# A hybrid decoder step on one core: where mixtures, inverses, the norm over heads and the residual's loads stand in their queues

## The chip, the cores and the metric

The kernel runs on one core of a Trainium2 chip. The metric is the device time of one execution in microseconds (us); lower is better. Before the change it is 2707.35 us, the median of three runs (2703.36 to 2710.01).

## The reference

One inference step of a two-layer decoder, all in float32: layer 0 mixes tokens with a causal convolution, layer 1 with an RWKV-7 recurrence, and each is followed by an MLP with squared ReLU. There is one prompt of 16 + 1024 tokens and a batch of 8 single tokens with states of their own. The part that matters here:

```python
def _rwkv7(h, ...):
    xx = prev - h                       # prev: h shifted by one token
    xr, xw, xk, xv, xa, xg = (h + xx * x_mix[i] for i in range(6))
    r, k, v = xr @ w_r, xk @ w_k, xv @ w_v
    ...                                 # decay, a, kk, gate g from small products
    S_final, ys = lax.scan(_wkv7_step, S0, xs)     # 64x64 state for each of 16 heads
    yn = (y - mu) * rsqrt(var + GN_EPS)            # norm over each head's 64 values
    out = ((yn + bonus) * g) @ w_o
    return out, h[:, -1], S_final

h = h + out
h = h + square(relu(rmsnorm(h) @ w_mlp_in)) @ w_mlp_out
```

## The kernel before, in words

Activations lie with features on the partitions and tokens along the free axis. Products of layer 0, of both MLPs and of `w_o` are made exact enough with three matmuls per 128x128 block: weights and activations are each split into a high part (a cast on ScalarE, L158 for weights `wi`, `wo`, L141 for activations) and a low part (a subtraction, on GpSimd L165 for weights, on VectorE L142 for activations); the matmuls are L190 to L192. Raw weights come through SP's DMA queue (L147), a few tiles ahead of use.

The program has these stages. (1) Layer 0's convolution and MLP for three groups of tokens, to about 1076 us. In the MLP, VectorE adds each finished bank `out` to the residual `h` (L357), and TensorE can't fill a bank again before that. (2) The projections of the recurrence layer, in four groups g of 272, 256, 256 and 264 tokens, to about 1750 us. `prepare(g)` loads the normalised rows `hx` (L861, L863) and forms `xx` (L868, two of three blocks on VectorE, the third on GpSimd); `mix` forms the mixture `mx` for one of the products and one block (L877). `keys(g)` makes the k products `pk` (L903), `mixer_in(g)` for each of 8 blocks p (two heads) the r and v products `pr`, `pv`, the small products `p_wa` (L974, L975), `l_w`, `l_a`, `l_g`, a scan over time of the decays (L1116) into `wa`, and the operands `ab` of the recurrence. PSUM banks of one kind come in a ring of four, those of the recurrence in a ring of three; a matmul waits for what reads the bank it takes.

(3) The recurrence in 17 chunks of 64 tokens (the first of 16), woven into stage 2 and the start of the last layer's MLP: for each chunk TensorE forms `A`, `gg`, `bT`, `W`, `po`, `U`, `S` and `Y` (L1236 to L1348), with VectorE and ScalarE between them. Each needs 32x32 triangular inverses, which `inverses(c, n)` (L1177 to L1209) works out for four chunks at once on VectorE: it loads `ni`, then alternates multiplications `tt` (L1197) and additions `ni` (L1200) on ever wider pieces. (4) For every two chunks, `norm_gate` (L1448 on): sums of `ey` over each head, mean and variance (L1459 to L1469), a transposition `yn` on TensorE (L1505), then gain, bonus and gate (L1484 to L1488) and a store to `d_z` (L1490). (5) `mixer_out(g)` for three groups of tokens of the last layer: products `ps_oo` of `z` with `w_o`, added to `h` (L1603) and squared (L252), and then the MLP.

The order is set by the order of the program, by a scheduler that moves instructions of all engines but TensorE, and by three kinds of hints. `kept_place(x)` keeps an instruction at its program position. `tc.issue_after(y)` queues an instruction behind a named one, `y`, of its engine. Generators stand for work that is woven in: `tick` takes one turn of the inverses, one of the recurrence and one of the norm, and each `yield` in them ends a turn, its number being a weight for `advance`. In stage 5 `filler` spreads three such streams over the points of the MLP: the rest of the recurrence (`until`), the decode step of the 8 single tokens, and the rest of the norm.

Memory comes from pools on a stack with two sides; a pool opened later on the same side gets what an earlier one gave back. The pool `wk` on the right holds the recurrence's tiles and also those of the norm. `lw.close()` gives it back; it stands behind the whole first MLP of the last layer with all its streams, and the residual `h` of groups 1 and 2 is loaded (`load_h`, L1581) into what it leaves. Four `wide` buffers hold the weights of the gate (`g`) and of the decay (`wa`), 24 `mixp` buffers the mixtures.

Of the kernel before, what the change touches and what calls it, by code (L numbers as in the profile page):

```python
# [16 lines left out]
P = 128  # L17
# [29 lines left out]
def hybrid_step(tc, x_prompt, x_sample, state_conv, state_shift, state_wkv, meta_tokens,  # L47
# [10 lines left out]
    with ctx:  # L58
# [244 lines left out]
        def filler(points, *streams):  # L303
# [10 lines left out]
            return fill, chain.from_iterable(it for it, _ in its)  # L314
        MLP_POINTS = 6 * DFF // P
# [5 lines left out]
        def mlp(layer, groups, lag, eng_w, eng_h, fill=None, done=None):  # L321
# [4 lines left out]
            hid = {}  # L326

# [9 lines left out]
            def inp(j, w, group):  # L337
# [5 lines left out]
                with tc.high_priority(offset=HR):  # L343
# [3 lines left out]
                    cur["low"] = split(hh[:, j % 2, :n], hl[:, j % 2, :n], s, eng_h)  # L347

            def out(b, i, w, group):
                gn, hv, n, ah, al, rs, hid_pool = group  # L350
                hh, hl = hid[gn, b]
                for m in range(4):
# [3 lines left out]
                    with tc.high_priority(offset=HA):  # L356
                        nc.vector.tensor_add(hv[:, 4 * i + m, :], hv[:, 4 * i + m, :], ps[:, :n])  # L357
# [422 lines left out]
        lw = ctx.enter_context(ExitStack())  # L780
        wk = pool(lw, "wk", 1, side="right")
# [30 lines left out]
        hnp = pool(ld, "hnp", 1)  # L812
        wide = pool(ld, "wided", 4)
        mixp = pool(ld, "mixp", 24)
# [14 lines left out]
        prep, norm, kept = {}, {}, {}  # L829
# [22 lines left out]
        def prepare(g):  # L852
# [13 lines left out]
            for k in range(KT):  # L866
                with nullcontext() if g else tc.issue_after(cur["low"].ins):
                    first = (nc.gpsimd if k % 3 == 2 else nc.vector).tensor_sub(xx[:, k, :npr], hx[:, k, 0:npr], hx[:, k, 1:1 + npr])  # L868
# [5 lines left out]
            def mix(i, k):  # L874

                t = mixp.tile([P, N1], F32, name=nm("mx", i, k), tag="mx")
                nc.vector.scalar_tensor_tensor(t[:, :n], xx[:, k, :n], vec("x_mix", i * KT + k), hx[:, k, 1:1 + n],  # L877
                                               op0=ALU.mult, op1=ALU.add)
# [59 lines left out]
        def mixer_in(g, tick):  # L938
# [140 lines left out]
            for p in range(KT):  # L1079
# [36 lines left out]
                nc.vector.tensor_tensor_scan(cum[:, :n], smask[:, :n], cum[:, :n], 0.0, op0=ALU.mult, op1=ALU.add)  # L1116
# [64 lines left out]
        def inverses(c, n):  # L1181
# [5 lines left out]
            (nc.sync if c else nc.gpsimd).dma_start(ni, blocks(d_n))  # L1187
            yield 5
            yield 1
            top = META if c == 0 else 32  # L1190
            every = 4 if c == 0 or c + n == NCH else 3 if c == 1 else 2
            aside = bank(f"tt{c}", "x")[:B] if c + n == NCH else None
            for j in range(top - 2, 0, -1):
# [3 lines left out]
                first = nc.vector.tensor_mul(o, ni[:, :j, j:j + 1].broadcast_to([B, j, wd]), ni[:, j:j + 1, j + 1:top].broadcast_to([B, j, wd]))  # L1197
                if j == top - 2:
                    kept_place(first)
# [10 lines left out]
        w_ = lambda shape, name, c, tag=None, bufs=1: wk.tile(shape, F32, name=f"{name}{c}", tag=tag or name, bufs=bufs)  # L1210
        kv = lambda t: t.rearrange("p (k v) -> p k v", k=KT)
# [60 lines left out]
        def chunk(c):  # L1272
# [67 lines left out]
            if c > 0:  # L1340
# [8 lines left out]
                ys[c] = w_([P, KT * HS], "ey", c, bufs=3)  # L1349
# [98 lines left out]
        def norm_gate():  # L1448
# [4 lines left out]
            def stats(y, n, name):  # L1453

                yv = y[:n].rearrange("t (h v) -> t h v", v=HS)
                ms = w_([P, 2, KT], "ems", name)
                sq = w_([P, KT * HS], "eq", name)
# [284 lines left out]
```

## Time and profile before

| | |
|---|---|
| median of three runs | 2707.35 us |
| profiled execution | 2701.97 us, its span 2700.3 us |
| granted TensorE clock, mean | 0.987 |
| TensorE busy | 2611.4 us, 97% |
| VectorE, ScalarE, GpSimd busy | 64%, 42%, 54% |
| DMA | 400.20 MB, 148 GB/s |

A row of a window shows its limits, its length, then the busy time of each engine with its number of instructions, the granted clock of TensorE (1.00 is full), the busy share of the DMA engines and what they moved. A row of a timeline shows start, time of one or several (x3) in a row, engine, line, operation and tiles, and in brackets how long the engine stood idle before it and what released it. A row of waits shows engine, what waited, for whom, and us in all, times, the longest. SPq is the queue of DMAs that SP issues; PE, DVE, ACT and POOL are TensorE, VectorE, ScalarE and GpSimd.

### The profile page before, as it was taken

Reading aid. Unit: us, or ns where it says so; the run is one execution under the profiler, and the core shown is the slowest. Engines: PE = TensorE matmul, PEld = TensorE weight load, DVE = VectorE, ACT = ScalarE, POOL = GpSimd, SP = SyncE. Lnnn points to the kernel's source line nnn. Section 1 sums busy time; section 2 is a strip of 40 time slices with the busy share of each in tenths; the row PEclk is TensorE's granted clock in tenths of the full one; section 3 lists DMA queues with packets and bytes.
Section 4 is the critical chain, followed back from the end, with each engine's and each line's share of the span. In section 5 each row is a group of like instructions: output and inputs, shape, how many; then the busy total and the mean of one; then the engine's idle time right before and its main releaser. Section 6 shows DMA issues by size and latency. Waiting matters only on the chain. (4 is left out here: it accounts for less than half of the span.)

```text
span 2700.3 us, 51347 instructions
## 1 busy us (share of the span) xinstructions
PE 2611.4 (97%) x19796; PEld 2455.6 (91%) x19796; DVE 1720.6 (64%) x3584; ACT 1134.6 (42%) x2099; POOL 1451.7 (54%) x2061
## 2 busy tenths in 40 slices
PE   9999999999999999998998999889999899999998
PEld 8999999999999999777887777789999899999998
DVE  6999999997444445344757476676679543334435
ACT  5546445445444333333344445445444442222223
POOL 7677878878887775022211113376678563333331
PEclk9999999999999999999999999999999999999999
DMA  6663544554456443568767867778655642222211
GB/s 187 175 167 108 161 145 134 155 175 133 141 160 187 138 141 107 171 196 211 198 175 188 213 154 194 189 197 191 154 163 175 178 124 70 71 71 71 64 54 44
DMA packets 602058, 400.20 MB, mean 148 GB/s; under 512 B 96128, under 2 KB 548928, under 8 KB 601814
## 3 DMA queue, kind: packets, MB, share of 16 engines
q1 hardware_dynamic: 573716, 359.95, 48.4%
q0 software_dynamic: 8768, 26.48, 3.1%
q10 hardware_dynamic: 19330, 10.49, 1.4%
q8 instruction: 156, 2.56, 0.4%
q14 instruction: 88, 0.72, 0.1%
HBM read 338.94 MB, written 58.83 MB: 147 GB/s over the span
## 5 line engine op out<-in xcount | busy, mean ns | idle before, releaser
L165 POOL TENSOR_TENSOR wo_lo<-wo_raw,wo_hi 128x256 fp32r<-128x256 f32 x736 | 540.7, 767 | 312.2 <-ACT wo_hi L158 302.7
L165 POOL TENSOR_TENSOR wi_lo<-wi_raw,wi_hi 128x256 fp32r<-128x256 f32 x640 | 472.1, 771 | 241.0 <-ACT wi_hi L158 235.5
L190 PE MATMUL out<-hh,wo_hi 128*128 128x352 f32 (+2 forms) x1536 | 498.7, 325 | 15.9 <-DVE h L357 11.4
L192 PE MATMUL ps_in<-m_l,wi_hi 128*128 128x352 f32 (+2 forms) x1536 | 492.9, 321 | 3.4 <-DVE m_l L288 3.4
L190 PE MATMUL ps_in<-m_h,wi_hi 128*128 128x352 f32 (+2 forms) x1536 | 494.5, 322 | 0.0
L357 DVE TENSOR_TENSOR h<-h,out 128x352 f32<-128x352 f32 (+2 forms) x768 | 385.8, 511 | 168.5 <-PE out L192 167.1
L191 PE MATMUL out<-hh,wo_lo 128*128 128x352 f32 (+2 forms) x1536 | 493.2, 321 | 0.0
L192 PE MATMUL out<-hl,wo_hi 128*128 128x352 f32 (+2 forms) x1536 | 492.1, 321 | 0.0
L191 PE MATMUL ps_in<-m_h,wi_lo 128*128 128x352 f32 (+2 forms) x1536 | 491.8, 320 | 0.0
L538 DVE SCALAR_TENSOR_TENSOR cv<-u,wdw,cv 128x348 f32<-128x348 f32 (+2 forms) x720 | 378.0, 575 | 0.7
L158 ACT CAST wi_hi<-wi_raw 128x1024 fp32r<-128x1024 f32 x160 | 167.7, 1049 | 386.9 <-PE out L192 192.6
L158 ACT CAST wo_hi<-wo_raw 128x1024 fp32r<-128x1024 f32 x184 | 192.6, 1048 | 325.5 <-PE out L192 166.2
L190 PEld LDWEIGHTS out<-hh,wo_hi 128*128 128x128 f32 x1536 | 289.8, 189 | 22.0 <-DVE h L357 13.7
L192 PEld LDWEIGHTS ps_in<-m_l,wi_hi 128*128 128x128 f32 x1536 | 288.6, 188 | 5.6 <-DVE m_l L288 5.2
L190 PEld LDWEIGHTS ps_in<-m_h,wi_hi 128*128 128x128 f32 x1536 | 289.5, 189 | 1.3
L191 PEld LDWEIGHTS out<-hh,wo_lo 128*128 128x128 f32 x1536 | 289.5, 188 | 0.8
L191 PEld LDWEIGHTS ps_in<-m_h,wi_lo 128*128 128x128 f32 x1536 | 289.1, 188 | 0.6
L192 PEld LDWEIGHTS out<-hl,wo_hi 128*128 128x128 f32 x1536 | 288.7, 188 | 0.0
L345 DVE SCALAR_TENSOR_TENSOR ps_in<-ps_in,rs_m 128x352 f32<-128x352 f32 (+2 forms) x192 | 100.6, 525 | 258.6 <-PE ps_in L192 258.3
L142 DVE TENSOR_TENSOR hl<-ps_in,hh 128x352 fp32r<-128x352 f32 (+2 forms) x192 | 98.8, 515 | 119.4 <-ACT hh L141 119.0
L346 ACT ACTIVATE ps_in<-ps_in 128x352 f32<-128x352 f32 (+2 forms) x192 | 85.1, 444 | 123.1 <-DVE ps_in L345 122.9
L903 PE MATMUL pv<-mx,wv_raw 128*128 128x256 f32 (+2 forms) x512 | 130.1, 403 | 1.1 <-ACT rk L1083 1.1
(368 smaller groups left out, 4677.5 us busy)
## 6 DMA issues: line engine op xcount, KB each, us to landing
wi_raw<-in_w_mlp_in_dram SPq DMA_DIRECT2D x160, 512.0 KB
wo_raw<-in_w_mlp_out_dram SPq DMA_DIRECT2D x160, 512.0 KB
wk_raw<-in_rwkv_w_k_dram SPq DMA_DIRECT2D x32, 512.0 KB
wr_raw<-in_rwkv_w_r_dram SPq DMA_DIRECT2D x32, 512.0 KB
wv_raw<-in_rwkv_w_v_dram SPq DMA_DIRECT2D x32, 512.0 KB
d_ab<-ab POOLq DMA_DIRECT2D x32, 512.0 KB, 4.3
pg_raw<-in_conv_w_pw_dram SPq DMA_DIRECT2D x24, 512.0 KB
pa_raw<-in_conv_w_pw_dram SPq DMA_DIRECT2D x24, 512.0 KB
```

The source lines that it names most:

```text
L142: return eng_lo.tensor_sub(lo, src, hi.bitcast(F32))
L158: cast = nc.scalar.copy(hi[:, :a * b], raw[:, :a * b])
L165: eng_lo.tensor_sub(lo[:, cs], raw[:, cs], hi[:, cs].bitcast(F32))
L190: nc.tensor.matmul(ps, w[0], act[0], start=first, stop=False)
L191: nc.tensor.matmul(ps, w[1], act[0], start=False, stop=False)
L192: nc.tensor.matmul(ps, w[0], act[1], start=False, stop=last)
L345: nc.vector.scalar_tensor_tensor(s, s, 0.0, rs()[:, :n], op0=ALU.max, op1=ALU.mult)
L346: nc.scalar.activation(s, s, AF.Square)
L357: nc.vector.tensor_add(hv[:, 4 * i + m, :], hv[:, 4 * i + m, :], ps[:, :n])
L538: nc.vector.scalar_tensor_tensor(acc[m][:, :n], ug[:, m, j:j + n], wdw[:, m, j:j + 1], acc[m][:, :n], op0=ALU.mult, op1=ALU.add)
L903: nc.tensor.matmul(ps[:, :n], w[:, k, :], act[k], start=k == 0, stop=k == KT - 1)
```

## The change

Line numbers of the changed kernel are up to 17 higher than before. No arithmetic is added or removed.

*Named places in the first MLP.* `mlp` records the low halves `hl` and the adds of `h`; `prepare(0)` queues its `xx` and mixtures behind them. Before, `xx0` stood behind the last `hl`, and the mixtures where the scheduler put them.

```diff
-                    cur["low"] = split(hh[:, j % 2, :n], hl[:, j % 2, :n], s, eng_h)
+                    low = split(hh[:, j % 2, :n], hl[:, j % 2, :n], s, eng_h)
+                    marks.setdefault(f"hl{gn}", []).append(low.ins)
...
-                        nc.vector.tensor_add(hv[:, 4 * i + m, :], hv[:, 4 * i + m, :], ps[:, :n])
+                        total = nc.vector.tensor_add(hv[:, 4 * i + m, :], hv[:, 4 * i + m, :], ps[:, :n])
+                    marks.setdefault(f"out{gn}", []).append(total.ins)
...
-                with nullcontext() if g else tc.issue_after(cur["low"].ins):
+                with nullcontext() if g else tc.issue_after(marks["hl2"][k + 5]):
                     first = (nc.gpsimd if k % 3 == 2 else nc.vector).tensor_sub(xx[:, k, :npr], ...
...
+                with nullcontext() if g else tc.issue_after(marks["out2"][2 * (k - KT) + 1 if i == 2 else -1]):
+                    nc.vector.scalar_tensor_tensor(t[:, :n], xx[:, k, :n], vec("x_mix", i * KT + k), hx[:, k, 1:1 + n], ...
```

VectorE's queue at the end of that MLP, before: `h0` is the residual, `out0_14_2_1` the bank for one block of it, `xx0` and `mx0_2_k` belong to the first group of the recurrence layer.

```order
L357 TENSOR_TENSOR h0_2_9300<-h0_2_9300,out0_14_2_1_12064 128x348
L868 TENSOR_TENSOR xx0_12375<-hx0_12372 128x272 x5
L357 TENSOR_TENSOR h0_2_9300<-h0_2_9300,out0_14_2_2_12072 128x348
L877 SCALAR_TENSOR_TENSOR mx0_2_0_12384<-xx0_12375,pvec_85,hx0_12372 128x272
L357 TENSOR_TENSOR h0_2_9300<-h0_2_9300,out0_14_2_3_12080 128x348
L877 SCALAR_TENSOR_TENSOR mx0_2_1_12386<-xx0_12375,pvec_85,hx0_12372 128x272
L877 SCALAR_TENSOR_TENSOR mx0_2_2_12388<-xx0_12375,pvec_85,hx0_12372 128x272
L877 SCALAR_TENSOR_TENSOR mx0_2_3_12390<-xx0_12375,pvec_85,hx0_12372 128x272
L357 TENSOR_TENSOR h0_2_9300<-h0_2_9300,out0_14_2_4_12097 128x348
```

The same place in VectorE's queue of the changed kernel:

```order
L360 TENSOR_TENSOR h0_2_9300<-h0_2_9300,out0_14_2_1_12064 128x348
L883 SCALAR_TENSOR_TENSOR mx0_2_0_12387<-xx0_12378,pvec_85,hx0_12375 128x272
L360 TENSOR_TENSOR h0_2_9300<-h0_2_9300,out0_14_2_2_12072 128x348
L360 TENSOR_TENSOR h0_2_9300<-h0_2_9300,out0_14_2_3_12080 128x348
L883 SCALAR_TENSOR_TENSOR mx0_2_1_12389<-xx0_12378,pvec_85,hx0_12375 128x272
L360 TENSOR_TENSOR h0_2_9300<-h0_2_9300,out0_14_2_4_12097 128x348
L661 SCALAR_TENSOR_TENSOR h0_1_132<-h0_1_132,pvec_85,st_d1_10699 128x348
L360 TENSOR_TENSOR h0_2_9300<-h0_2_9300,out0_14_2_5_12106 128x348
L883 SCALAR_TENSOR_TENSOR mx0_2_2_12391<-xx0_12378,pvec_85,hx0_12375 128x272
```

The `xx0` have left this place for six single ones behind earlier `hl`; one mixture follows every two adds, and those for the other products follow the last add.

*Inverses behind the scan.* The first multiplication of a set of inverses is queued behind the first scan of the next group instead of being kept at its program place, and the load of `ni0` goes from GpSimd's queue to SP's.

```diff
+                scans.setdefault(g, scan.ins)
...
-            (nc.sync if c else nc.gpsimd).dma_start(ni, blocks(d_n))
+            nc.sync.dma_start(ni, blocks(d_n))
             yield 5
             yield 1
+            group = next((g for g in range(4) if CHUNKS[g][0] > max(c, 1)), None)
+            while group and group not in scans:
+                yield 1
...
-                if j == top - 2:
-                    kept_place(first)
+                with tc.issue_after(scans[group]) if group and j == top - 2 else nullcontext():
+                    nc.vector.tensor_mul(o, ...)
```

VectorE's queue at the first of these, before: `wa1_0` is the scan of group 1's first block, `tt0`, `ni0` the inverse of the first chunk.

```order
L142 TENSOR_TENSOR r16l1_13737<-r161_13735,r16h1_13736 128x256
L1197 TENSOR_TENSOR tt0_14_13747<-ni0_13727 32x14
L1200 TENSOR_TENSOR ni0_13727<-ni0_13727,tt0_14_13747 32x14
L1197 TENSOR_TENSOR tt0_13_13750<-ni0_13727 32x26
...
L1197 TENSOR_TENSOR tt0_10_13802<-ni0_13727 32x50
L1116 SCALAR_TENSOR_TENSOR wa1_0_13784<-smask1_13606,wa1_0_13784 128x256
```

VectorE's queue there in the changed kernel, on to the operation `rk21_0` whose bank the prediction speaks of:

```order
L142 TENSOR_TENSOR r16l1_13740<-r161_13738,r16h1_13739 128x256
L1122 SCALAR_TENSOR_TENSOR wa1_0_13778<-smask1_13609,wa1_0_13778 128x256
L1208 TENSOR_TENSOR tt0_14_13821<-ni0_13730 32x14
L1209 TENSOR_TENSOR ni0_13730<-ni0_13730,tt0_14_13821 32x14
L1208 TENSOR_TENSOR tt0_13_13824<-ni0_13730 32x26
L1141 TENSOR_TENSOR wa1_0_13778<-st1_0_12851,wa1_0_13778 128x256
L1209 TENSOR_TENSOR ni0_13730<-ni0_13730,tt0_13_13824 32x13x2
L873 TENSOR_TENSOR xx2_13867<-hx2_13819 128x256
L1144 SCALAR_TENSOR_TENSOR rk1_0_13814<-rk21_0_13752,pvec_85,wa1_0_13778 128x256
L873 TENSOR_TENSOR xx2_13867<-hx2_13819 128x256
L1208 TENSOR_TENSOR tt0_12_13827<-ni0_13730 32x36
L873 TENSOR_TENSOR xx2_13867<-hx2_13819 128x256 x3
L1121 SCALAR_TENSOR_TENSOR rk21_0_13752<-st1_0_12851,negs_12324,pb1_0_13800 128x256
```

The scan now stands ahead of the inverse; `xx2` for the next group still stands ahead of `rk21_0`.

*The norm's turns and memory.* The norm's tiles (`ey`, `ems`, `eq`, `ez`, `ebv`, `egt`) come from a pool `wn` of their own, with the same numbers of buffers; ahead of the first `yn` of each two chunks stand two more turns; and the order of the pools `mixp` and `wide` is swapped.

```diff
+        wn = pool(ctx, "wn", 1, side="right")
         wk = pool(lw, "wk", 1, side="right")
...
+        mixp = pool(ld, "mixp", 24)
         wide = pool(ld, "wided", 4)
-        mixp = pool(ld, "mixp", 24)
...
                     yield 3
+                    if not hf:
+                        yield 1
+                        yield 1
                     pt = bank(f"yn{c}_{hf}", "w")
```

*The residual in mid-MLP.* The stream that ends the recurrence goes on to give back its memory and to load `h` of groups 1 and 2.

```diff
+            def next_h():
+                lw.close()
+                residp2 = pool(l1, "resid2", 2, **right)
+                for g in (1, 2):
+                    load_h(g, residp2, wide)
+                yield 1
...
-                                ([until(NCH - 1)], FA * CHUNK_WAIT * (NCH - 1 - st["done"]) + INV),
+                                ([until(NCH - 1), next_h()], FA * CHUNK_WAIT * (NCH - 1 - st["done"]) + INV),
...
-            lw.close()
             outp = pool(l1, "outp", 1)
-            residp2, actp2, hidp2 = pool(l1, "resid2", 2, **right), ...
-            for g in (1, 2):
-                load_h(g, residp2)
+            actp2, hidp2 = pool(l1, "actp2", 1, **right), pool(l1, "hidp2", 2, **right)
```

SP's queue at these loads, before: `wo1_7` is a block of `w_o`, `d_z` the norm's output of the single tokens, `zr20` the first `z` of group 2.

```order
L147 DMA wo1_7_raw_24259<-in_rwkv_w_o_dram 128x8x128
L1490 DMA d_z_80<-egt1040_0_23850 128x4x8
L1475 DMA ebv1040_1_23974<-d_bv_77 128x4x8
L1490 DMA d_z_80<-egt1040_1_23975 128x4x8
L1581 DMA h1_1_24005<-d_h_73 128x8x352
L1581 DMA h1_2_24007<-d_h_73 128x8x352
L1593 DMA zr20_24404<-d_z_80 128x2x352
```

SP's queue where they stand in the changed kernel: `wi1_0_18` is block 18 of 32 of the MLP's first weight, `out_4` the recurrence's final state.

```order
L147 DMA wo1_0_7_1_raw_22491<-in_w_mlp_out_dram 128x2x512
L1378 DMA out_4_dram<-fo16_22096 128x8x64
L147 DMA wi1_0_18_raw_22532<-in_w_mlp_in_dram 128x8x128
L1594 DMA h1_1_22141<-d_h_73 128x8x352
L1594 DMA h1_2_22143<-d_h_73 128x8x352
L147 DMA wi1_0_19_raw_22587<-in_w_mlp_in_dram 128x8x128
```

The two loads of `h` have moved from behind the last store of the norm to behind the recurrence's last store, with 13 of the 32 blocks of that MLP still to come.

36 lines of the change are left out of this document (19 added, 17 removed).

## The prediction

> **What bounds the kernel now.** I read the page first: how full TensorE is decides what can be won at all.
>
> ```profile
> span 2700.3 us, 51347 instructions
> PE 2611.4 (97%) x19796; PEld 2455.6 (91%) x19796; DVE 1720.6 (64%) x3584; ACT 1134.6 (42%) x2099; POOL 1451.7 (54%) x2061
> ```
>
> TensorE works 2611.4 of 2700.3 us, and the change takes no matmul away. So 88.9 us of idle time, and what the halved clock costs behind it, is all there is to win. I then cut the span into windows and kept those where TensorE is idle and the change moves something; after the first few places the window is set on the stretches whose granted clock is halved.
>
> ```profile
> core 0: us, PE busy (x) PEld busy (x) DVE busy (x) ACT busy (x) POOL busy (x), PEclk, DMA share, GB/s
> 1070.00:1081.50 11.50, 7.06 (x42) 6.20 (x40) 11.50 (x28) 2.11 (x5) 1.00 (x1) 1.00 0.69 215
> 1081.50:1088.30 6.80, 5.32 (x17) 3.64 (x18) 2.42 (x6) 1.92 (x5) 0.93 (x1) 0.53 0.61 190
> 1271.00:1276.10 5.10, 3.01 (x14) 2.30 (x13) 0.78 (x5) 0.00 (x0) 0.14 (x1) 1.00 1.08 297
> 1276.10:1286.30 10.20, 5.71 (x12) 3.72 (x13) 9.68 (x36) 3.90 (x11) 1.54 (x3) 0.52 0.50 141
> 1437.00:1440.10 3.10, 0.40 (x2) 0.14 (x1) 3.10 (x11) 2.48 (x8) 0.00 (x0) 1.00 0.94 195
> 1440.10:1450.20 10.10, 5.75 (x16) 3.91 (x17) 9.60 (x24) 2.21 (x4) 0.91 (x2) 0.51 0.23 56
> 1600.00:1650.00 50.00, 44.01 (x466) 35.59 (x466) 38.90 (x100) 21.68 (x54) 11.16 (x23) 0.90 0.55 141
> 1720.00:1860.00 140.00, 123.70 (x1412) 111.50 (x1411) 101.94 (x204) 71.09 (x141) 85.94 (x115) 0.95 0.74 189
> 2110.00:2122.70 12.70, 9.28 (x64) 8.62 (x62) 3.17 (x9) 3.48 (x12) 0.00 (x0) 1.00 0.29 67
> 2122.70:2132.90 10.20, 5.26 (x17) 4.88 (x18) 1.38 (x3) 4.10 (x6) 5.38 (x8) 0.51 0.71 239
> ...
> 1960.00:2000.00 40.00, 38.31 (x281) 37.32 (x280) 25.51 (x54) 18.70 (x33) 28.04 (x37) 1.00 0.56 155
> ...
> 2200.00:2600.00 400.00, 400.00 (x2506) 399.94 (x2505) 164.47 (x317) 101.45 (x162) 146.99 (x208) 1.00 0.25 74
> ```
>
> Each pair is an idle stretch and the slow stretch behind it: PEclk falls to about 0.5 for 6.8 or 10.2 us. A stall is therefore priced as its idle time plus half of what TensorE works at half clock. The last row, TensorE full, gives 400 / 2506 = 0.16 us for a matmul of the MLP. I call the places C (1070), D (1271), E (1437), F (1600), G (1720) and J (2110).
>
> **The change part by part.** Times of other instructions are those of before; the code is re-timed along them.
>
> *C, the mixtures.* At the end of the first layer's MLP VectorE owes TensorE one add of `h` per bank of `out`.
>
> ```profile
> PE out L190 <- DVE h L357: 3.2, 2, 1.6
> PE st_d L241 <- POOL acc_d L263: 2.8, 1, 2.8
> 1069.69 2.14 DVE L877 SCALAR_TENSOR_TENSOR mx<-xx,pvec,hx 128x272 f32<-128x272 f32 x5
> 1075.95 2.56 DVE L877 SCALAR_TENSOR_TENSOR mx<-xx,pvec,hx 128x272 f32<-128x272 f32 x6
> 1081.61 1.36 DVE L357 TENSOR_TENSOR h<-h,out 128x348 f32<-128x348 f32 x3
> ```
>
> Runs of five and six mixtures stand between adds (0.43 us a mixture), so the last adds end at 1083.0 and TensorE waits 3.2 + 2.8 us. Idle is (11.50 - 7.06) + (6.80 - 5.32) = 5.9 us, clock 5.32 / 2 = 2.7 us. After the change the six `xx0` stand far ahead in the MLP, and at most one mixture stands per two adds: 2 x 0.43 + 0.43 = 1.3 us of VectorE, against six matmuls at 0.16 us for each `out`, 1.9 us for two. VectorE keeps up, and the other 16 mixtures come after the last add; their products start only after the 64 of the first key block. The swap of the two pools moves the loads of `g0` and `wa0` to the end of the MLP in SP's queue; they too are needed only some 30 us after the transition, so I cost them at nothing (late, they would stall `p_g` by what they lack). I leave 0.5 us for the last `st_d`. Gain 8.1 us, between 6 (a wait like the 2.8 us one stays in part) and 8.6.
>
> *D, the first inverse.* VectorE's queue:
>
> ```profile
> 1275.18 0.16 DVE L1197 TENSOR_TENSOR tt<-ni 32x14 f32<-32x14 f32 x1 [13.21 <-DMA ni<-d_n]
> 1279.42 1.22 PE L1102 MATMUL l_w<-lwa,wa 64*128 64x256 f32 x2 [5.42 <-ACT vv L1108]
> 1281.29 0.46 DVE L1115 SCALAR_TENSOR_TENSOR rk<-st,negs,pb 128x256 f32<-128x256 f32 x1
> 1281.80 1.22 PE L1102 MATMUL l_a<-lwa,wa 64*128 64x256 f32 x2 [1.16 <-DVE rk L1115]
> 1276.62 0.61 POOL L868 TENSOR_TENSOR xx<-hx 128x256 f32<-128x256 f32 x1 [1.27 <-DMA hx<-d_hn]
> ```
>
> VectorE stands 13.2 us for `ni0`, and the scan, the exponentials and the copy of `vv` stand behind it; TensorE waits for its bank. With the scan first, `l_w` can start when the matmuls ahead of it end, at 1279.42 - 5.42 = 1274.0. But `l_a`, the next matmul, takes the bank that `rk21_0` (L1115) frees, and in the new queue five `xx2` stand ahead of that one. They need `hx2`, which lands at 1276.6, or some 0.4 us later since `ni0` now goes through SP ahead of it. 1277.0 + five subtractions (0.36 each) + three other operations and `rk` (1.1) gives 1279.9 for `l_a`, against 1281.80: 1.9 us. The clock still halves behind an idle time of 5.3 us. Then the last `xx2` and eight `mx2_2` (0.41 each) come at 1287.2 to 1291; `pk2_0`, which starts 8 us after `l_a` in before, arrives at 1287.9, so 1 to 1.5 us are given back; a 0.9 us wait of `A` that follows in before goes, its matmuls being later. I take 1.3 us; bounds -2 (the mixtures late by their full chain) and 4 (`hx2` early).
>
> *E, the norm in group 2.*
>
> ```profile
> 1438.23 0.33 PE L1505 MATMUL yn<-ident,ey 128*128 128x128 f32 x1 [1.17 <-ACT gg L1295]
> 1444.45 0.90 PE L1505 MATMUL yn<-ident,ey 128*128 128x128 f32 x3 [5.88 <-DVE ey L1469]
> 1440.57 2.91 DVE L877 SCALAR_TENSOR_TENSOR mx<-xx,pvec,hx 128x264 f32<-128x264 f32 x7
> 1426.79 0.59 PE L975 MATMUL p_wa<-hx,wa_raw 128*128 128x256 f32 x2
> 1427.42 0.54 SPq L863 DMA_DIRECT2D hx<-d_hn  x1
> 1435.25 1.39 POOL L868 TENSOR_TENSOR xx<-hx 128x256 f32<-128x256 f32 x2 [12.21 <-DMA hx<-d_hn]
> ```
>
> `yn` waits 1.17 + 5.88 us, the longer one behind seven mixtures and inverse steps. Idle 2.70 + 4.35 = 7.05 us, clock 5.75 / 2 = 2.9 us. Two more turns put `yn1_0` behind `pk3_0`, `W3` and `po3`, about 11 us later, when `ey2` is done. What is late next: `hx3` is issued when `p2_wa` ends (1427.42 behind 1426.79) and lands 7.8 us later; `p2_wa` now ends 3 us earlier, since chunk 2's `S`, `Y` and `A34` stand behind it, so `xx3` opens at 1432.2. Behind `xx3` in VectorE's queue stands `rk22_0`, done at 1435.0, whose bank `A341` takes: arrival 1433.3, wait 1.7. Then `pv2_1` waits for a copy of `rk22_1` queued behind `eq2` on ScalarE: 1.6 us. C shows a halved clock behind waits of 1.6 to 2.8 us, so I charge one 3.4 us stretch, 1.7. Gain 7.05 + 2.9 - 3.3 - 1.7 = 5.0, between 2 (both halve it and the waits double) and 8.
>
> The Trainium skill ("TensorE: Matmul & The Clock Gate", Part 1: The HAM clock gate) has the clock go to half only after at least one whole idle window of about 3.4 us. The stretch at 1081.5 speaks against that: the longest wait ahead of it is 2.8 us, and the clock is 0.53. By the page E would gain 6.7 us, by the row 5.0.
>
> *F and G, groups 2 to 3 and the start of the last layer.*
>
> ```profile
> PE yn L1505 <- DVE ey L1469: 1.5, 1, 1.5
> PE A L1236 <- ACT uv L1330: 2.7, 1, 2.7
> PE Y L1346 <- DVE nr L1246: 4.6, 1, 4.6
> ```
>
> F is idle for 6.0 us and G for 16.3. The same extra turns take `yn`'s 1.5 us; `ni9`'s 30 steps, now behind group 3's first scan, run beside later chunks instead. The waits for `uv` and `nr` are of recurrence steps that only change place. I take 1.5 us for F (bounds -4, two waits like `A`'s 2.7 with some clock, and 6, all of its idle), and nothing for G: bounds -6 and 6, one wait like the 4.6 with its clock added or gone.
>
> *J, the residual `h` of groups 1 and 2.*
>
> ```profile
> 2117.74 0.19 DVE L1488 TENSOR_TENSOR egt<-ebv,egt 128x32 f32<-128x32 f32 x1
> 2118.49 1.84 SPq L1581 DMA_DIRECT2D h<-d_h  x2
> 2125.46 1.38 DVE L1603 TENSOR_TENSOR h<-h,ps_oo 128x352 f32<-128x352 f32 x3 [7.52 <-DMA h<-d_h]
> 2126.01 0.50 ACT L252 ACTIVATE sq<-h 128x352 f32<-128x352 f32 x1 [8.53 <-DVE h L1603]
> 2127.49 0.66 PE L190 MATMUL ps_oo<-z_h,wo_hi 128*128 128x352 f32 x1 [8.22 <-ACT wo_hi L158]
> 1972.97 3.41 SPq L147 DMA_DIRECT2D wi_raw<-in_w_mlp_in_dram  x2
> ```
>
> The memory of `h` is that of the recurrence and of the norm, whose last use is at 2117.74; the loads go out at 2118.49, VectorE waits for them, ScalarE's squares for VectorE, the casts of `wo` stand behind the squares, and TensorE waits 8.2 us for those casts. With the norm in its own pool both loads stand behind `wi1_0_18` on SP, near 1975, some 140 us before use. They are 2.9 MB; what is queued behind them is the MLP's weights, five loaded and five split tiles ahead, each good for 24 matmuls of 0.16 us, so some 38 us. The row from 1960 to 2000 has the DMA engines 0.56 busy at 155 GB/s; the rest of them, about 120 GB/s, moves 2.9 MB in 24 us, so nothing waits. Idle 8.2 + clock 5.26 / 2 = 10.8 us. Next in line are the `z` loads of group 2, which move up with the casts that free their buffers. Bounds 8 (`z` late by a part) and 11.
>
> *Sum.* 8.1 + 1.3 + 5.0 + 1.5 + 0 + 10.8 = 26.7 us. From the profiled execution, 2700.3 us of span and 1.7 around it (2702.0), that gives 2675.3. That run lies 5.4 us below the median of the three timed ones, 2707.35, so for a median I say 2707.35 - 26.7 = **2680.6 us**. All lower bounds together give a gain of 6 - 2 + 2 - 4 - 6 + 8 = 4 us (2703), all upper ones 8.6 + 4 + 8 + 6 + 6 + 11 = 44 us (2664).
>
> **The rivals.**
>
> First: the recurrence's moved steps pay for D, E and F. Every chunk's `A`, `gg`, `W` and `S` now stand one turn later, against other work of VectorE; the waits of 2.7 and 4.6 us above show that such meetings cost. Then only C and J remain: 2707.35 - 18.9 = 2688. For it: D's own working above keeps most of the wait. Against it: VectorE is 64% busy and what is moved is not more.
>
> Second, on the other side: the same mechanism in nearly each of the 16 full chunks. From a mean loss of 1.7 us a chunk (26.7 / 16) all gain is gone, from 2.2 it is slower by over 0.3%; half of the loss of one wait like `A <- uv` with its clock, (2.7 + 1.7) / 2 = 2.2, is enough in the mean, and 2.3 gives 2707.35 - 26.7 + 36.8 = 2717. For it: every such step crosses VectorE's queue twice. Against it: in E only two waits of 1.7 us arise, and behind `hx3` VectorE waits for no load of this phase again.
>
> Third, the change doesn't do what it says in J: the two loads wait on SP for the last chunk's readers, and hold the weights queued behind them. Against it, `fo`, the last chunk's output, is stored just ahead in that queue. If J comes to nothing and half of the rest holds, 15.9 / 2, the time is 2699.
>
> Fourth, short waits leave the clock alone: E gives 1.7 us more, and the time is 2679. It is the page's rule above that would do this; the row at 1081.5 speaks against it.
>
> **How the numbers follow.** About 0.3%, 8.1 us, is what a measurement of this kernel can tell from no change. Forecast 0.56, first rival 0.20, second 0.09, third 0.05, fourth 0.10. Range 2664 to 2703: the bounds above, which take in every rival but the second. Faster by over 0.3% (under 2699.2): 0.54 + 0.16 + 0.03 + 0.10 = 0.83; within: 0.02 + 0.04 + 0.02 + 0.01 = 0.09; slower: 0.08, all of the second rival.
>
> **What would show it.** C right: no wait of `out` for `h` over 0.5 us and PEclk 1.00 at the transition. D: `l_a` waits 4 to 6 us for `rk`, and VectorE's `xx` waits for `hx`; if `l_a` starts with `l_w`, my bank rule is wrong. E: `yn` without a wait, `A` and `pv` with 1 to 2 us each. J: `h` adds without a DMA wait and no `ps_oo` wait over 1 us. F and G: the idle time of 6.0 and 16.3 us changes by less than 6. The prediction is wrong if new waits on VectorE stand in the stretch 1290 to 1860 for over 10 us more than now, or if `wi` loads starve TensorE behind the two `h` loads.

## The result and the profile after

The changed kernel takes 2678.51 us (median of four runs, 2677.32 to 2680.24) against 2707.36 us for the kernel before beside it: a ratio of 0.9895, 95% interval 0.9878 to 0.9912. Forecast were 2680.6 us. The profiled execution took 2680.24 us, against 2701.97 us for that of before: 21.7 us, less than the 28.9 us between the medians, since before's profiled run lies 5.4 us under its median and this one 1.7 us over. In the later sessions the median of before was 2701.8 to 2704.3 us, so a gain of 25 us is as good a reading as one of 29.

The page of the changed kernel, its span and its first row:

```profile
span 2678.5 us, 51360 instructions
PE 2602.9 (97%) x19796; PEld 2450.6 (91%) x19796; DVE 1725.7 (64%) x3584; ACT 1132.7 (42%) x2097; POOL 1450.9 (54%) x2060
```

TensorE is idle for 75.6 us instead of 88.9, and its busy time is 8.5 us shorter with as many matmuls, which is mostly the halved clock gone. The same places in windows (length, busy time of each engine, granted clock, DMA):

```profile
core 0: us, PE busy (x) PEld busy (x) DVE busy (x) ACT busy (x) POOL busy (x), PEclk, DMA share, GB/s
1060.00:1080.00 20.00, 19.82 (x123) 19.04 (x121) 14.68 (x30) 5.98 (x12) 5.10 (x7) 1.00 0.54 167
1080.00:1100.00 20.00, 19.88 (x90) 16.07 (x91) 13.75 (x28) 4.58 (x12) 0.00 (x0) 1.00 0.79 231
1263.00:1276.70 13.70, 8.29 (x38) 6.74 (x38) 4.61 (x14) 4.40 (x12) 1.74 (x3) 0.92 1.02 251
1276.70:1283.40 6.70, 6.30 (x20) 4.82 (x20) 6.32 (x25) 2.60 (x7) 0.88 (x2) 0.66 0.25 83
1300.00:1400.00 100.00, 95.88 (x1010) 77.77 (x1010) 71.00 (x175) 38.98 (x102) 18.61 (x33) 1.00 0.74 189
1415.00:1450.00 35.00, 30.09 (x284) 24.39 (x283) 25.70 (x64) 15.88 (x35) 5.37 (x7) 0.95 0.63 175
1591.00:1641.00 50.00, 43.99 (x539) 35.67 (x539) 35.36 (x86) 19.19 (x49) 14.18 (x21) 0.97 0.48 122
1702.00:1842.00 140.00, 127.78 (x1602) 115.68 (x1597) 108.07 (x221) 69.67 (x145) 85.75 (x116) 0.95 0.86 202
2080.00:2110.00 30.00, 27.94 (x177) 26.42 (x177) 24.59 (x49) 17.31 (x37) 17.36 (x22) 1.00 0.55 142
2110.00:2135.00 25.00, 25.00 (x159) 25.00 (x158) 13.33 (x23) 14.83 (x26) 22.18 (x28) 1.00 0.70 195
```

The transition (C) and the residual (J) run at full clock with next to no idle time. The first inverse (D) still has 13.70 - 8.29 = 5.4 us of idle time and a slow stretch behind it. F (from 1591) is idle for 6.0 us as before, at a clock of 0.97 instead of 0.90, and G (from 1702) for 12.2 instead of 16.3. One stretch has got worse, the one from 1300 to 1400. Its row in the kernel before, for which TensorE is busy throughout:

```profile
1300.00:1400.00 100.00, 100.00 (x1116) 82.00 (x1111) 65.68 (x161) 44.72 (x115) 18.05 (x32) 1.00 0.75 191
```

The longest of TensorE's waits in the changed kernel (what waits, for what; sum, times, longest):

```profile
PE out L190 <- DVE hl L142: 10.2, 5, 5.4
PE pb L803 <- ACT vv L1114: 7.0, 8, 1.7
...
PE ps_oo L192 <- DVE z_l L142: 5.8, 2, 5.2
PE l_a L1108 <- DVE rk L1121: 5.8, 1, 5.8
...
PE A L1246 <- DVE nr L1256: 4.0, 3, 1.9
PE pv L909 <- ACT rk L1089: 3.6, 3, 2.7
```

Gone are the waits for the casts of `wo` (8.2 us), for `ey` (5.9) and of `l_w` for `vv` (5.4). New are `l_a` for `rk`, one of 5.4 us for `hl`, and one of 5.2 us of `ps_oo`, at the start of the last layer, for `z_l` (the low half of `z`). The last stands behind an inverse. VectorE and TensorE there:

```profile
1741.90 0.21 DVE L1208 TENSOR_TENSOR tt<-ni 128x30 f32<-128x30 f32 x1 [4.80 <-DMA ni<-d_n]
1742.02 2.01 DVE L142 TENSOR_TENSOR z_l<-zr,z_h 128x328 fp32r<-128x328 f32 x2
...
1743.14 0.64 PE L192 MATMUL ps_oo<-z_l,wo_hi 128*128 128x328 f32 x1 [5.19 <-DVE z_l L142]
```

`tt` is the first multiplication of the last set of inverses. No later group has a scan for it to stand behind, so the edit leaves it without a place; it stands ahead of the fourth `z_l` and waits there 4.80 us for the load of `ni`. In the kernel before it comes at 1766 and waits for nothing. All eight kernels with the inverses' edit have this wait of `ps_oo`, of 4.8 to 6.3 us; of those without it none has more than 0.5 us.

**The lost time by stage.** To compare kernels whose stages stand at different times, I cut each trace into windows of 1.67 us and add up, from one matmul to the next stage's, the idle time plus busy time x (1 - PEclk). Each column is one profiled run.

| lost, us | before | changed | a_turns | a_inv | u_turns | u_inv | u_port |
|---|---|---|---|---|---|---|---|
| up to 855 | 10.1 | 9.9 | 10.1 | 11.3 | 10.4 | 11.9 | 10.6 |
| 855 to 880 (`nmask`) | 3.5 | 7.2 | 4.3 | 5.8 | 1.8 | 4.6 | 4.0 |
| transition (C) | 8.8 | 0.3 | 10.1 | 8.9 | 0.3 | 0.3 | 0.3 |
| group 0 | 3.4 | 5.0 | 5.1 | 3.5 | 4.9 | 5.0 | 4.9 |
| group 1 (D) | 10.5 | 13.0 | 12.5 | 11.9 | 14.0 | 12.2 | 11.1 |
| group 2 (E) | 12.4 | 9.0 | 5.3 | 10.3 | 10.5 | 8.4 | 9.0 |
| group 3 (F, G) | 22.3 | 16.1 | 24.8 | 21.2 | 20.7 | 23.0 | 19.3 |
| last layer, 320 us (G) | 17.1 | 20.1 | 17.4 | 17.1 | 13.5 | 15.5 | 19.2 |
| the rest (J) | 16.0 | 3.3 | 19.0 | 15.7 | 4.9 | 4.8 | 3.4 |

The first row, which no edit touches, differs by 2 us between kernels. Other cells spread more. Up to 1438 us a_turns has the order of before on TensorE, VectorE, ScalarE and GpSimd, and loses 1.3, 1.7 and 2.0 us more in the transition and in groups 0 and 1. The kernel a_resid (below), with that order up to 1980 us, loses 1.6 us less in group 2 and 3.3 less in group 3 than before. So a difference of up to 3 us in one cell is not told from the spread between executions. The profiled runs of a_turns and a_inv also lie 4.9 and 4.1 us above the medians of these kernels. From before to the changed kernel the cells add up to 104.1 - 83.9 = 20.2 us, of the 21.7 between the two profiled runs.

### The profile page after: what moved, and what is told of

It is laid out like the page before. It is cut to its first block, busy times and chain, and to the rows that moved or that the text cites. A ratio compares the mean times of both kernels' runs of the same rounds, so it can differ in the third digit from the quotient of the medians.

```text
span 2678.5 us, 51360 instructions
## 1 busy us (share of the span) xinstructions
PE 2602.9 (97%) x19796; PEld 2450.6 (91%) x19796; DVE 1725.7 (64%) x3584; ACT 1132.7 (42%) x2097; POOL 1450.9 (54%) x2060
## 4 chain that ended last, share of the span: by engine, by line
PE 79%; DVE 11%; DMA 3%; ACT 2%; issue 2%; POOL 2%; SPq 0%; ACTq 0%; DVEq 0%; POOLq 0%
PE out L190 8%; PE ps_in L190 8%; PE ps_in L192 8%; PE ps_in L191 8%; PE out L191 8%; PE out L192 8%; PE pk L909 4%; PE pr L909 3%; PE pv L909 2%; DVE tt L1208 1%; DVE ni L1209 1%; PE ps_g L190 1%; PE ps_o L192 1%; PE ps_g L191 1%; PE ps_g L192 1%
## 5 line engine op out<-in xcount | busy, mean ns | idle before, releaser
L1074 POOL DMA_DIRECT2D d_n<-n x32 | 24.3, 760 | 217.5 <-DVE n L1064 112.4
```

## The experiments

The theory: the gain consists of parts that add up, C and J above all, with smaller ones for the inverses and for the norm's turns. The rival: in the recurrence the moved steps give back what they win, so the turns or the inverses bring nothing. First each part alone on the kernel before; then the whole without one part; then, from what the trace showed, two versions that go on.

**a_resid**, the norm's pool and the early residual alone:

```diff
+        wn = pool(ctx, "wn", 1, side="right")
...
+                                ([until(NCH - 1), next_h()], FA * CHUNK_WAIT * (NCH - 1 - st["done"]) + INV),
```

> The kernel before with one part alone: the norm's tiles in their own pool and the loads of h for groups 1 and 2 in mid-MLP. My theory: only the place at 2110 to 2133 us changes. The wait of ps_oo for wo_hi (8.2 us) and the halved clock behind it go, and the waits of the z loads after it shrink, so 11 to 13 us less, 2694 to 2697 where before is 2707; the MLP ahead of it loses at most 1 us to the two loads. Rival (the gain of the whole change at that place hangs on the recurrence ending earlier, which the other parts bring): 5 us or less, and a wait of some ps_in or out for wi or wo around the two loads.

Measured: 2689.68 us, ratio 0.9954 (0.994 to 0.9967), 12 us. In the changed kernel SP's row of the loads and VectorE's rows of the adds tell why. The loads go out 156 us before the first add that uses them:

```profile
1946.09 2.48 SPq L1594 DMA_DIRECT2D h<-d_h  x2
```

and no add waits for a DMA, VectorE now waits for TensorE:

```profile
2101.97 0.51 DVE L1616 TENSOR_TENSOR h<-h,ps_oo 128x352 f32<-128x352 f32 x1
...
2109.52 0.52 DVE L1616 TENSOR_TENSOR h<-h,ps_oo 128x352 f32<-128x352 f32 x1 [2.40 <-PE ps_oo L192]
```

**a_marks**, the mixtures by their marks and the order of the two pools alone:

```diff
-                with nullcontext() if g else tc.issue_after(cur["low"].ins):
+                with nullcontext() if g else tc.issue_after(marks["hl2"][k + 5]):
...
+                with nullcontext() if g else tc.issue_after(marks["out2"][2 * (k - KT) + 1 if i == 2 else -1]):
```

> The kernel before with one part alone: xx0 and the mixtures of group 0 queued behind named instructions of the first MLP, and the pools mixp and wide in the other order. My theory: the transition at 1060 to 1130 us gets 8 to 9 us shorter (no wait of out for h over 0.5 us, st_d under 0.5 us, full clock), nothing else changes, 2698 to 2699. Rival (the loads of g0 and wa0, moved to the end of the MLP, come late and the products p_g or p_wa wait): 3 us or less.

Measured: 2695.24 us, 0.9967 (0.9955 to 0.998), 8.9 us. VectorE at the transition of the changed kernel:

```profile
1070.00 0.50 DVE L883 SCALAR_TENSOR_TENSOR mx<-xx,pvec,hx 128x272 f32<-128x272 f32 x1
1070.52 0.52 DVE L360 TENSOR_TENSOR h<-h,out 128x348 f32<-128x348 f32 x1
1071.46 0.52 DVE L360 TENSOR_TENSOR h<-h,out 128x348 f32<-128x348 f32 x1 [0.43 <-PE out L192]
...
1079.99 0.50 DVE L360 TENSOR_TENSOR h<-h,out 128x348 f32<-128x348 f32 x1
1080.42 7.09 DVE L883 SCALAR_TENSOR_TENSOR mx<-xx,pvec,hx 128x272 f32<-128x272 f32 x17
```

One mixture stands between two adds, VectorE waits for `out`, and the run of seventeen comes behind the last add.

**a_inv**, the inverses behind the scans, and `ni0` on SP, alone:

```diff
-            (nc.sync if c else nc.gpsimd).dma_start(ni, blocks(d_n))
+            nc.sync.dma_start(ni, blocks(d_n))
...
+                with tc.issue_after(scans[group]) if group and j == top - 2 else nullcontext():
```

> The kernel before with one part alone: the first multiplication of each set of inverses queued behind the next group's first scan, and ni0 loaded by SP. My theory: l_w no longer waits (5.4 us), but l_a waits 4 to 6 us for rk, which stands behind xx2 and so behind the load of hx2; 1 to 3 us are gained at 1270 to 1300 and the recurrence's steps, which move, give back as much up to 1460: within 3 us of before. Rival (the stall at 1271 is taken away whole): 8 us less.

Measured: 2699.05 us, 0.9986 (0.9977 to 0.9995), some 4 us, a little more than the 3 of the theory. TensorE's longest waits in group 2 (1421 to 1596) of this kernel:

```profile
PE pb L798 <- ACT vv L1108: 3.7, 3, 2.2
PE A L1239 <- DVE fs L1357: 1.6, 1, 1.6
PE pv L903 <- ACT rk L1083: 1.6, 2, 1.0
```

The wait of `yn` for `ey` (5.9 us before) is not among them: it goes with the inverses, without any extra turn. In group 3 the 4.6 us wait of `Y` goes too, but others take its place: `pb` waits 6.0 us in all there, and at the start of the last layer `ps_oo` 5.6 us for `z_l`, as in the changed kernel.

**a_turns**, the two turns ahead of the first `yn` alone:

```diff
+                    if not hf:
+                        yield 1
+                        yield 1
```

> The kernel before with one part alone: two more turns ahead of the first yn of each two chunks. My theory: the yn waits at 1437 to 1450 (7.05 us and the clock behind them) and at 1615 (1.5 us) go, 1 to 4 us come back as waits of A or pv for work queued on VectorE and ScalarE: 4 to 8 us less. Rival (the norm's stages only meet VectorE's queue one place later): yn waits as long as before, within 2 us.

Measured: 2701.76 us, 0.9996 (0.9987 to 1.0005): no gain. Group 2 loses 7.1 us less, and no wait of `yn` is left, as the theory has it. What groups 0 and 1 lose more stands ahead of the first `yn`, where the order is that of before: this is the spread. Group 3 loses 2.5 us more. TensorE's waits in group 3 of this kernel (1592 to 1758):

```profile
PE Y L1346 <- DVE nr L1246: 5.2, 2, 4.6
PE pb L798 <- ACT vv L1108: 3.9, 3, 1.9
PE gg L1287 <- DVE nr L1246: 3.4, 1, 3.4
```

The 3.4 us of `gg` are new there. In time the rival holds for the turns; where the rest of the 7.1 us is given back, one profiled run does not tell. The four parts alone, (1 - ratio) x 2704 us, add up to 12.4 + 8.9 + 3.8 + 1.1 = 26 us, of 28 for the whole.

**u_turns**, the changed kernel without the two turns (the diff above, backwards).

> The changed kernel without the two more turns of the norm. Alone they gave 0.9996, though yn's wait at 1437 went. Theory A (the turns pay only beside the inverses' move, since the steps they meet are those that it shifts): 4 us or more slower than the whole change, 2682 or more where the whole has 0.9895 of before, and a yn wait of 3 us or more in 1400 to 1460. Theory B (the turns only push the norm's waits to other places of VectorE's queue): within 2 us of the whole change, 0.9888 to 0.9902.

Measured: 2675.23 us, 0.9899 (0.9884 to 0.9914): the turns bring nothing in the whole either, and `yn` does not wait without them. With them groups 2 and 3 lose 1.5 and 4.6 us less and the last layer 6.6 us more.

**u_inv**, the changed kernel without the inverses' part (the diff of a_inv, backwards).

> The changed kernel with the inverses and the load of ni0 as they were before (kept at their program place, ni0 on GpSimd's queue). Theory A: the inverses behind the scan bring in the whole what they bring alone, about 4 us; without them the ratio to the kernel before is 0.9895 + 0.0014 = 0.991 (0.990 to 0.992), and l_w waits 5 us for vv again. Theory B: what they save at the first inverse (the long wait shrinks little: 5.4 us for vv become 5.8 us for rk) is given back by the small new waits of group 1's recurrence; the ratio stays at 0.9885 to 0.990 and TensorE's busy share between 1300 and 1400 us rises again.

Measured: 2684.03 us, 0.993 (0.9917 to 0.9943), 5.5 us slower than the whole by the medians, 9 by the ratios of the two sessions. By the time this is theory A, and more than it asked; but not where it said. Group 1 loses 12.2 us against 13.0, so the first inverse brings nothing that shows. Group 3 loses 23.0 against 16.1, the last layer 15.5 against 20.1; the wait of `ps_oo` for `z_l` is absent there. VectorE at the end of group 3 in u_inv, and the durations of all of that line (shortest, median, longest):

```profile
1731.07 0.49 DVE L1121 SCALAR_TENSOR_TENSOR rk<-st,negs,pb 128x264 f32<-128x264 f32 x1 [0.49 <-PE pb L803]
1731.60 3.05 DVE L1141 TENSOR_TENSOR wa<-rk,wa 128x264 f32<-128x264 f32 x1
...
L1141 DVE TENSOR_TENSOR wa<-rk,wa x32: 406/426/3053, 1141.4 to 1731.6; 128x256 f32<-128x256 f32 x16, 128x272 f32<-128x272 f32 x8, 128x264 f32<-128x264 f32 x8
```

GpSimd beside it:

```profile
1731.78 2.10 POOL L165 TENSOR_TENSOR wo_lo<-wo_raw,wo_hi 128x256 fp32r<-128x256 f32 x3
1733.82 0.57 POOL L1081 DMA_DIRECT2D d_bv<-bv  x1
1734.41 0.82 POOL L165 TENSOR_TENSOR wo_lo<-wo_raw,wo_hi 128x256 fp32r<-128x256 f32 x1
```

and TensorE behind it:

```profile
1737.76 1.97 PE L1353 MATMUL Y<-sv,xa 128*64 128x64 f32 x32 [4.55 <-DVE nr L1253]
```

The product takes 3.05 us, with a median of 0.43 for its line, and ends when GpSimd's three subtractions and the DMA issue behind them are over. `nr`, queued behind it, keeps TensorE waiting 4.55 us. The kernel before has the same: 3.06 us at 1736.95, and the 4.6 us wait of `Y` that the prediction quotes; so have a_resid, a_marks and a_turns. The changed kernel, a_inv and u_turns have it not.

**u_port** tests this cause: u_inv, with those four subtractions put behind the product. The orders of VectorE and TensorE are those of u_inv; on SP one load of a block of `w_o` comes four loads later.

```diff
-                eng_lo.tensor_sub(lo[:, cs], raw[:, cs], hi[:, cs].bitcast(F32))
+                with tc.issue_after(made[7]) if name == "wo0_0" else nullcontext():
+                    eng_lo.tensor_sub(lo[:, cs], raw[:, cs], hi[:, cs].bitcast(F32))
...
-                        dd(p, i, src)
+                        made[p] = dd(p, i, src).ins
```

> The changed kernel with the inverses as before (u_inv), and in it the four GpSimd subtractions wo_lo of the last layer's first block of w_o put behind the two small GpSimd copies that wait for VectorE's product wa<-rk,wa of the recurrence's last block; VectorE's and TensorE's orders are those of u_inv. In before, a_turns and u_inv that product takes 3.05 us instead of 0.43, beside these subtractions, and Y behind it waits 4.6 us for nr; in a_inv, after and u_turns it does not. Theory A (in the whole the inverses bring their time in group 3 because VectorE's queue then meets GpSimd's subtractions at another moment, and the stretched product is what costs): the product takes under 0.6 us, the wait of Y shrinks from 4.6 to under 2.5 us, and the ratio goes from u_inv's 0.993 to 0.9905 to 0.992. Theory B (the product is long for another reason, or Y waits for something else that the inverses free): the product or the wait stays and the ratio stays at 0.9925 to 0.9935.

Measured: 2678.31 us, 0.9901 (0.9884 to 0.9917). VectorE's product:

```profile
1729.59 0.43 DVE L1143 TENSOR_TENSOR wa<-rk,wa 128x264 f32<-128x264 f32 x1
```

GpSimd's subtractions, now behind it:

```profile
1731.24 2.77 POOL L167 TENSOR_TENSOR wo_lo<-wo_raw,wo_hi 128x256 fp32r<-128x256 f32 x4
```

and TensorE:

```profile
1732.61 1.15 PE L1355 MATMUL Y<-sv,xa 128*64 128x64 f32 x32 [1.41 <-DVE nr L1255]
```

Theory A holds for the product, which is back at 0.43 us, and for the wait, at 1.41. The time is at the level of the whole, a little under theory A's range, and its interval ends where that of u_inv begins. So the subtractions make the product long and `Y` wait. That this is what the inverses' part brings in the whole is not shown: against u_inv, group 3 loses 3.7 us less in the profiled runs and the last layer 3.7 more, with a new wait of 2.95 us of `ps_oo` for `wo_hi`. Where the 5.7 us between the medians of u_inv and u_port come from stays open.

**u_swap**, the changed kernel with the two pools in their old order:

```diff
-        mixp = pool(ld, "mixp", 24)
         wide = pool(ld, "wided", 4)
+        mixp = pool(ld, "mixp", 24)
```

> The changed kernel with the pools mixp and wide in the order of before, so that the first loads of the wide pool do not wait for the end of the MLP. The prediction cost the swap at nothing. Theory A (the swap costs nothing and brings nothing): ratio 0.988 to 0.991. Theory B (the six mixtures that now start in the MLP need the memory that the swap gives them early; without it they come late and the transition waits again): ratio 0.991 to 0.993 with a wait of out or p_k above 2 us at the transition.

Measured: 2676.02 us, 0.9897 (0.9882 to 0.9913): the swap does nothing.

**f_nmask** goes on from the changed kernel. Its new wait of 5.4 us of `out` for `hl`, from 862.6 on, has this in front of it on VectorE:

```profile
863.63 3.64 DVE L774 TENSOR_SCALAR nmask<-m_ar,par32q 128x32 f32<-128x32 f32 x1 [4.22 <-DMA m_ar<-m_ar]
...
867.47 0.51 DVE L142 TENSOR_TENSOR hl<-ps_in,hh 128x348 fp32r<-128x348 f32 x1
```

and on GpSimd this:

```profile
861.69 5.54 POOL L165 TENSOR_TENSOR wo_lo<-wo_raw,wo_hi 128x256 fp32r<-128x256 f32 x8
```

The kernel before has the same instruction with 0.51 us:

```profile
864.30 0.51 DVE L770 TENSOR_SCALAR nmask<-m_ar,par32q 128x32 f32<-128x32 f32 x1 [3.79 <-DMA m_ar<-m_ar]
```

The experiment builds `nmask` by GpSimd and copies `m_ar` on ScalarE's queue:

```diff
-        nc.sync.dma_start(m_ar[HS:, :], m_ar[:HS, :])
+        nc.scalar.dma_start(m_ar[HS:, :], m_ar[:HS, :])
...
-        nc.vector.tensor_scalar(nmask, m_ar[:, :32], par32[:, 0:1], None, op0=ALU.mult)
-        nc.vector.scalar_tensor_tensor(nmask, m_ar[:, 32:HS], par32[:, 1:2], nmask, op0=ALU.mult, op1=ALU.add)
+        for q in range(4):
+            qs = slice(32 * q, 32 * q + 32)
+            nc.gpsimd.tensor_copy(nmask[qs], m_ar[qs, 32 * (q % 2):32 * (q % 2) + 32])
```

> The changed kernel with m_ar's lower half copied by a DMA from ScalarE's queue instead of SP's, and nmask made by four copies on GpSimd instead of two operations on VectorE. Theory A (the multiplication of nmask, 3.4 to 3.6 us in the kernels with the marks and 0.3 to 0.6 us in the others, waits for GpSimd's subtractions of wo_lo, and all of VectorE's adds wait behind it): the wait of out for hl at 861 to 867 (5.4 us) and the halved clock behind it go, 5 to 8 us less than the whole change, 0.9866 to 0.9877. Theory B (that wait is the load of m_ar or TensorE's own, and nmask is late with it): 2 us or less.

Measured: 2670.54 us, 0.9882 (0.9866 to 0.9898). The stretch 855 to 880 loses nothing any more, but the whole gains only 3.5 us by ratio on the changed kernel, less than expected. That stall is not in every execution: u_swap, with the changed kernel's order on all four engines, has `nmask` at 0.87 us and loses 4.9 us in this stretch, where the profiled run of the changed kernel loses 7.2.

**f_xx** puts the five `xx` that wait for `hx` behind the last product of the block before, so that `rk` is not queued behind them:

```diff
-                with nullcontext() if g else tc.issue_after(marks["hl2"][k + 5]):
+                with (tc.issue_after(made[g - 1]) if k % 3 < 2 else nullcontext()) if g else tc.issue_after(marks["hl2"][k + 5]):
...
-                if g and k in (0, 2):
+                if g and k == 2:
                     kept_place(first)
```

> The changed kernel with the xx of groups 1 to 3 on VectorE queued behind the operands ab of the block before, instead of standing ahead of rk. My theory (l_a waits for a bank that rk frees, and rk stands behind xx and so behind the load of hx): the wait of l_a at 1271 to 1277 (5.8 us) and the clock behind it go, and the A wait of 1.6 us at 1430; pk then waits 1 to 3 us for the mixtures: 3 to 7 us less than the whole change, 0.987 to 0.9884. Rival (the load of hx is what bounds: pk2_0 now waits for the mixtures by as much as l_a did): within 2 us of the whole change.

Measured: 2664.32 us, 0.9862 (0.9843 to 0.9882), 9 us better than the changed kernel, more than the 3 to 7 forecast. Group 1 loses 8.9 us instead of 13.0, group 2 7.0 instead of 9.0.

**f_both**, the last two together.

> The changed kernel with both of the last two edits. If they are two places that don't touch: the sum of their two differences to the whole change, 8 to 15 us less, 0.984 to 0.9866; if the recurrence takes back what it finds: not under 0.9866.

Measured: 2661.16 us, 0.9847 (0.9831 to 0.9863), the best version. Its VectorE at the first inverse:

```profile
1263.76 2.94 DVE L874 TENSOR_TENSOR xx<-hx 128x256 f32<-128x256 f32 x6 [4.10 <-DMA hx<-d_hn]
...
1270.03 0.67 DVE L1123 TENSOR_TENSOR_SCAN wa<-smask,wa 128x256 f32<-128x256 f32 x1
```

The load of `hx` still decides there: the next block's scan stands behind `xx` and eight mixtures, and `pb` waits 5.0 us for `vv` behind it. The wait of `ps_oo` for `z_l` is still there too, with 6.3 us; no run puts the last set of inverses alone back in its old place.

**f_lean**, f_both without the two turns.

> The best version so far (nmask by four GpSimd copies, xx of groups 1 to 3 on VectorE behind the block before) without the two turns ahead of the first yn. Theory A (the turns bring nothing in any surrounding): 0.984 to 0.9855, as with them (0.9847). Theory B (with the xx out of the way the turns at last keep what they win in group 2): 0.986 to 0.9875, 4 to 7 us slower than with them.

Measured: 2661.45 us, 0.9847 (0.9833 to 0.986): the turns bring nothing here either.

## Why the prediction was right, point by point

*C* was right: 8.1 us forecast, 8.5 in the transition's cell, 8.9 alone. No wait of `out` is left there, `st_d` waits 0.3 us, the clock is 1.00, and the pool swap costs nothing (u_swap).

*J* was right and a little small: 10.8 us forecast, 12.7 in its cell, 12.4 alone. What was taken for next in line, the `z` loads, is not late.

*D* was right in its mechanism. VectorE in the changed kernel:

```profile
1264.13 0.69 DVE L1122 TENSOR_TENSOR_SCAN wa<-smask,wa 128x256 f32<-128x256 f32 x1 [6.50 <-ACT wa L1111]
...
1273.62 0.42 DVE L873 TENSOR_TENSOR xx<-hx 128x256 f32<-128x256 f32 x1 [7.90 <-DMA hx<-d_hn]
...
1276.58 0.46 DVE L1121 SCALAR_TENSOR_TENSOR rk<-st,negs,pb 128x256 f32<-128x256 f32 x1
```

and TensorE:

```profile
1277.10 1.22 PE L1108 MATMUL l_a<-lwa,wa 64*128 64x256 f32 x2 [5.81 <-DVE rk L1121]
```

The scan runs at once, `l_a` waits 5.8 us for the bank of `rk`, and that stands behind `xx` and its load, link by link as forecast. But the waits of `l_w` and `l_a` together shrink only from 6.6 to 5.8 us, and group 1 as a whole loses 2.5 us more than before, where 1.3 less were forecast. The step that failed is the one that let 1 to 1.5 us be given back: between 1300 and 1400 some 4 us of small waits arise. It is the inverses' edit that makes them: `pb` waits there for `vv` three times, 2.0 us in all (1.9 in a_inv), in the changed kernel, a_inv, u_turns and u_swap, and not at all in before, a_resid, a_turns, u_inv and u_port. The 2.5 us themselves are within the spread.

*E* has about the right size, by luck. Group 2 loses 3.4 us less, 5.0 forecast. The new waits came: `A` 1.6 us (1.7 forecast, though it is for `fs`), `pv` 2.7 and `pb` 1.5 where 1.6 stood. The failed step is "Two more turns put `yn1_0` behind `pk3_0`, `W3` and `po3`", as the reason of the gain: alone the turns do take `yn`'s wait away (a_turns), but the inverses' edit does so without them (a_inv, u_turns). The price put on the turns is one of the inverses, too: `A` and `pv` wait as long or nearly so in a_inv (1.6, 1.6) and u_turns (1.4, 3.2), and not in group 2 of a_turns and u_inv. The quoted sentence on the row had the other reason in it: `ey` stood behind mixtures "and inverse steps", and the change moves those.

*F and G* were too small: 1.5 + 0 forecast, 6.2 - 3.0 = 3.2 us in their two cells, inside the bounds and no more than the spread. The 4.6 us wait of `Y` was taken for one of "recurrence steps that only change place". It was that of a product lengthened beside GpSimd, a row that the prediction did not look at. It goes, but G, put at nothing, has the new 5.2 us wait of `ps_oo` for `z_l` in its place. Against the second rival the prediction held that behind `hx3` VectorE waits for no load of this phase again; it waits 4.80 us for `ni`.

Not in the sum at all were 3.7 us of `nmask` and 1.6 us in group 0, on the losing side, of which the order need not be the cause: a_turns loses as much in group 0 with the order of before. So the sum of 26.7 us is right as a total through errors that partly cancel: by the cells, 8.5 (C) - 2.5 (D) + 3.4 (E) + 3.2 (F, G) + 12.7 (J) - 5.1 (the two unforeseen and the first row) = 20.2 us for the profiled pair, where it said 26.7; the medians of the session, 28.9 us apart, then lie on the other side.

Of the rivals, the first holds in part (the turns, group 1), the second and third do not: TensorE's waits on VectorE between 1290 and 1860 come to 19.9 us instead of 24.7, and the `h` loads starve no weight. The fourth falls: from 1415 to 1450 the longest wait is 2.7 us and the granted clock 0.95, which is 30.09 x 0.05 = 1.5 us lost, as charged (1.7). The Trainium skill ("TensorE: Matmul & The Clock Gate", Part 1: The HAM clock gate) asks for a whole idle window of about 3.4 us first; this trace does not agree. The waits of 0.9 to 1.1 us between 1300 and 1400 leave the clock at 1.00.

## What to carry to other kernels

When a change has several parts, run each alone and the whole without each: here the turns, to which the prediction gave 5 us, bring nothing, and the inverses bring next to nothing at the wait that they were moved for and make a new one of 5.2 us some 470 us behind it. Before a wait is put down to the order of a queue, compare the durations of the instructions in front of it with others of their line (median against maximum): here one at seven times its usual length was a collision, and moving four instructions of another engine took it away. Where a queue holds work that waits for a load, put it behind all that does not; that (f_xx) was worth 9 us beyond the change. And where a hint that keeps an instruction in its place is replaced, look at the cases that get no new place.

## What the runs showed of the hardware

VectorE operations are now and then stretched beside GpSimd's runs of subtractions: `wa<-rk,wa` 3.05 us instead of 0.43, `nmask` 3.64 instead of 0.33 to 0.87. Both end within 0.3 us of the end of a run of several GpSimd instructions (eight `wo_lo`, until 867.23; three and a DMA issue, until 1734.39), not of the first of them. The product is long in all five kernels that keep the old order of that step and of the subtractions (before, a_resid, a_marks, a_turns, u_inv), and u_port shows that the subtractions cause it. The `nmask` case is long in two of eleven profiled runs with that instruction, and its cause is only argued from the coinciding ends. The Trainium skill ("SBUF — State Buffer", Who interferes with whom) has VectorE operations with two SBUF inputs, or in a fast mode, and GpSimd's shut each other out of a shared port for one instruction. That fits the partners of the product, which has two inputs; whether `nmask` runs in such a mode no run shows. That the wait lasts over several instructions of the other side is not in it.
